# Encoder block on Trainium2: block sums for part of the down projection, and a rearranged output projection

## The chip, the core and the metric

The kernel runs on one core of a Trainium2 chip. A core has TensorE (PE, matrix products into PSUM), VectorE (DVE), ScalarE (ACT), GpSimd (POOL) and SyncE (SP). Each engine works through its own list of instructions in order and waits on semaphores for the others; SP, ACT and POOL also issue DMAs, each on its own queue. The metric is the device time of one execution in microseconds (us), as the median of several runs.

## The reference

One layer of a transformer encoder in fp32: 2048 positions of width 1024. Four heads of differential attention and four groups of Fourier mixing share an input and an output projection, and a gated MLP of width 2816 with a convolution over three positions follows.

```python
h = rmsnorm(x, g_mix[l]);  z = h @ w_in[l]
o_da = diff_attention(q, k, v, lam, slopes)          # from slices of z
o_da = rmsnorm(o_da, g_subln[l], SUBLN_EPS) * (1.0 - lambda_init)
o_ft = fourier_mix(u, w_ft[l])
x = x + concatenate([o_da, o_ft]) @ w_out[l]          # output projection
h = rmsnorm(x, g_ffn[l])
up = centred_dwconv(h @ w_up[l], w_conv[l], b_conv[l])
gate, val = up[..., :D_FF], up[..., D_FF:]
x = x + (jax.nn.silu(gate) * val) @ w_down[l]         # down projection
return rmsnorm(x, g_final)
```

## The kernel before

Every fp32 product is made of three matmuls in the fp32r type. `split` (L79) cuts an operand into a rounded upper part (ACT copy, L83, "hi") and the rest (a subtraction on DVE, or on POOL where `lo_engine` says so, L84, "lo"); `mm3` (L121) then issues hi*hi (L127), hi*lo (L128) and lo*hi (L129). So each operand costs an ACT and a DVE (or POOL) step before PE can use it, and the unit of PE's work is a matmul over 512 columns. A norm is `rstd` and a scaling: ACT squares and sums (L97), POOL adds the epsilon and takes the power (L100, L102), DVE scales (L709 where the result is `hn` or `y`).

The stages follow one another: input projection (to about 330 us), Fourier mixing and attention (to about 985 us), output projection (`out_proj`, L711, to about 1199 us), and the MLP. Positions are cut into 16 blocks (NB) of 128, the 2816 channels into 22 f tiles (NF) of 128.

`out_proj` goes over the 16 blocks. `fetch` brings the mixed rows (mt) and their head scales (fr), `load` multiplies them on POOL (L733) and splits the two halves (ms), lo of the one on POOL, of the other on DVE; `half` makes the products with w_out (tiles wo, wo_x) and adds the residual x (L753); `close` normalises the block before, `transposes` turns the result (hn) by PE (L766) between two groups of matmuls, and ACT stores it to `htd` in DRAM. The weights w_out are split in `out_weights`, lo on DVE, from the end of attention on. `scale_rows` turns the head scales (fs, from POOL at L635) by a PE transpose (L701) and puts them into DRAM for `fetch`; for the last four blocks this is called at block 1. From block 9 on, `b_pieces` (L848) runs beside it in steps: it loads the transposed rows again (hb), forms the block sums that the up projection needs (`sums`, L822 to L825, on POOL), splits them into operands (b) and stores two of the sums (bd).

The up projection is done by block sums (the Strassen-Winograd scheme): a 2 x 2 block product takes 7 products, p1 to p7, instead of 8. Positions go in two groups of 1024. For each group and each f tile there are 7 products of 4 x 3 matmuls = 84. The seven sums of the activations (the b slots, `bops`) are made once per group; the sums of the weights (`sums`, L816 to L819, on DVE) are made for each tile. Products are added up in PSUM banks a, c and d, which other engines read between two products. Convolution, SiLU and the product of gate and value follow, and the result goes to `gd` in DRAM, laid out as [f tile][channel][position].

The down projection is plain. A round handles 512 positions: for each of the 22 f tiles, w_down's rows (512 KB) and the gate columns (256 KB) are loaded, split (tiles d), and multiplied for 4 blocks x 2 column halves, 24 matmuls in 8 PSUM banks that stay open over the round (`down_mm`). At its end `down_out` loads the residual (y<-x2d, L1025), adds it (L1028), normalises and stores to the output (L1033). A round is 528 matmuls, and there are four.

What sets the order: `ffn` lists slots (products and f tiles): up group 0, down round 0, up group 1, down rounds 1, 2, 3. `flow` (L1046) walks through them and issues splits up to three slots ahead and loads a little further, into a ring of 9 operand tiles and two stage tiles. The operands of up group 1 are made by `b_part` during round 0. The last 8 f tiles of round 3 (`LATE`) are prepared in the then unused b slots, and their products run bank by bank, so that the blocks finish one after the other. A scheduler then orders each engine's list by its own model, and the program runs these lists as they are.

Of the kernel before, what the change touches and what calls it, by code (L numbers as in the profile page):

```python
# [40 lines left out]
class Block:  # L41
# [3 lines left out]
    def __init__(self, ctx, tc, a):  # L45
# [22 lines left out]
        self.gd = dt("gd", [NF, P, S], F32)  # L68
# [445 lines left out]
    def out_weights(self, sp, slot, kb, part=0, tag="wost"):  # L514
# [196 lines left out]
    def out_proj(self, pieces):  # L711
# [3 lines left out]
        with ExitStack() as es:  # L715
# [14 lines left out]
            def load(tb):  # L730
# [3 lines left out]
                for half in (1, 0):  # L734
                    m2 = p.tile([P, 4, 2, P], F32R, tag="ms", bufs=4, name=f"ms{tb}_{half}")
                    self.split(mt[:, 4 * half:4 * half + 4], m2[:, :, 0, :], m2[:, :, 1, :],
                               lo_engine=nc.gpsimd if half else None)
# [5 lines left out]
            def half(tb, half, between=None):  # L743
# [8 lines left out]
                self.mm3(ps, [term(kb) for kb in range(H)], first=False)  # L752
                return nc.vector.tensor_tensor(x2[:, c], ps, x2[:, c], ALU.add)  # L753

            def close(tb):
                ms, x2 = ready.pop(tb)
                hn = p.tile([P, D], F32, tag="xh", bufs=4, name=f"hn{tb}")
                self.norm(p, hn, x2, gffn, f"h{tb}", hn)
# [19 lines left out]
            load(0)  # L778
            for _ in self.out_weights(w, lambda: w.tile([P, 1, 2, D], F32R, name="wo3"), H - 1, tag="g"):
# [3 lines left out]
            for tb in range(NB):  # L783
                if tb + 2 < NB:
                    fetch(tb + 2)
                transposes = close(tb - 1) if tb > 0 else None
                half(tb, 0)
                if tb == 1:
                    self.scale_rows(p, pst.tile([P, HALF], F32, tag="tp", name="fsr"), H - 1, NB - 4)
# [17 lines left out]
    def sums(self, pool, blocks, name, eng, last=False):  # L807
# [4 lines left out]
        new = lambda n: pool.tile([P, HALF], F32, tag="sum", bufs=3, name=f"{name}_{n}")  # L812
        t1, t2, t4 = new("t1"), new("t2"), new("t4")
        tt = eng.tensor_tensor
        if not last:
# [16 lines left out]
    def b_part(self, grp, kb, out):  # L832
# [3 lines left out]
        st = self.stage(f"hb{grp}_{kb}")  # L836
        t0 = grp * S // 2
        for half in range(2):

            nc.sync.dma_start(  # L840
                st[:, half::2], self.htd[kb + 4 * half, :, t0:t0 + S // 2].rearrange("p (n t) -> p n t", n=2))
        x11, x21, x12, x22 = (st[:, i] for i in range(4))

        t1, t2, t3, t4 = self.sums(self.sp, (x11, x21, x12, x22), f"hs{grp}_{kb}", nc.vector, True)
# [3 lines left out]
    def b_pieces(self, out):  # L848
# [18 lines left out]
        for kb in range(4):  # L867
            x11, x21, x12, x22 = st[kb]
            t1, t2, t3, t4 = self.sums(self.sp, (x11, x21, x12, x22), f"hs0_{kb}", nc.gpsimd, True)
# [5 lines left out]
            nc.sync.dma_start(self.bd[0, :, kb], t3)  # L875
            nc.sync.dma_start(self.bd[1, :, kb], t4)
# [19 lines left out]
    def up_slots(self, grp):  # L896

        out = [(0, "p1")]
        for n in range(NF):
            out += [(n, q) for q in ("p5", "p6", "p2", "p7")]  # L900
            if n + 1 < NF:
                out.append((n + 1, "p1"))
            out += [(n, "p4"), (n, "p3")]
        return [("up", grp, n, q) for n, q in out]

    def load_up(self, grp, n):
# [297 lines left out]
```

## Time and profile before

| | us |
|---|---|
| median of 3 runs | 2544.21 |
| runs, lowest to highest | 2540.18 to 2544.71 |
| profiled execution | 2540.28 |
| span of its trace | 2538.5 |
| output projection, about 985 to 1199 | 214 |
| up group 0, about 1199 to 1615 | 416 |
| down round 0, about 1615 to 1743 | 128 |
| up group 1, about 1743 to 2163 | 420 |
| down rounds 1 to 3, about 2163 to 2530 | 367 |

The profiled execution is one among several; its own time and its span differ by 1.8 us, which lie outside the trace. Stage bounds are read from the trace and are rounded. The first part of the profile's page gives busy time and share of each engine; the rows of windows give busy time by stage; the rows of waits give an engine, what it waited for, the total, the number of times and the longest. A row of a group gives line, engine, operation, output<-input, shape and count, and behind the bar the busy time in us, the mean ns of one, and the idle time ahead of it with what ended it. The clock column is the share of PE's full clock that was granted.

### The profile page before, as it was taken

Reading aid. Unit: us, or ns where it says so; the run is one execution under the profiler, and the core shown is the slowest. Engines: PE = TensorE matmul, PEld = TensorE weight load, DVE = VectorE, ACT = ScalarE, POOL = GpSimd, SP = SyncE. Lnnn points to the kernel's source line nnn. Section 1 sums busy time; section 2 is a strip of 40 time slices with the busy share of each in tenths; the row PEclk is TensorE's granted clock in tenths of the full one; section 3 lists DMA queues with packets and bytes.
Section 4 is the critical chain, followed back from the end, with each engine's and each line's share of the span. In section 5 each row is a group of like instructions: output and inputs, shape, how many; then the busy total and the mean of one; then the engine's idle time right before and its main releaser. Section 6 shows DMA issues by size and latency. Waiting matters only on the chain.

```text
span 2538.5 us, 34822 instructions
## 1 busy us (share of the span) xinstructions
PE 2484.4 (98%) x13037; PEld 2113.0 (83%) x13037; DVE 1668.7 (66%) x2595; ACT 1301.0 (51%) x2036; POOL 716.9 (28%) x792
## 2 busy tenths in 40 slices
PE   9999998999999998989999999999999999999998
PEld 9998877888888887867888888877888888888886
DVE  4533358988889995343977777667878777434443
ACT  6322236888888884333645545445455455333332
POOL 1400014898888885261110110100001000000000
PEclk9999999999999999999999999999999999999999
DMA  7335558343241215675322222444222222546463
GB/s 266 98 121 145 149 153 227 78 76 76 45 104 28 55 34 173 207 231 182 112 83 92 75 83 88 162 161 171 86 89 75 86 90 87 187 143 218 154 204 111
DMA packets 147080, 317.53 MB, mean 125 GB/s; under 512 B 12432, under 2 KB 65760, under 8 KB 140000
## 3 DMA queue, kind: packets, MB, share of 16 engines
q1 hardware_dynamic: 87088, 231.88, 27.0%
q0 software_dynamic: 18816, 37.72, 7.1%
q10 hardware_dynamic: 41008, 45.72, 5.8%
q8 instruction: 102, 1.67, 0.3%
q14 instruction: 66, 0.54, 0.1%
HBM read 231.34 MB, written 83.93 MB: 124 GB/s over the span
## 4 chain that ended last, share of the span: by engine, by line
PE 46%; DVE 2%; DMA 2%; ACT 1%; issue 1%; POOL 0%; SPq 0%; POOLq 0%; ACTq 0%; DVEq 0%
PE pd L127 5%; PE pd L129 4%; PE pd L128 4%; DMA wd<-in_w_down 1%; DVE d L84 1%; DVE b L84 1%; DMA hb<-htd 1%; DMA wd<-gd 0%; PE pu_0a L127 0%; DVE y L1028 0%; PE pu_21a L127 0%; PE pu_21a L129 0%; PE pu_19a L129 0%; PE pu_15a L129 0%; PE pu_7a L127 0%
## 5 line engine op out<-in xcount | busy, mean ns | idle before, releaser
L592 POOL TENSOR_TENSOR z<-z,z 128x1024 f32<-128x1024 f32 x128 | 307.1, 2416 | 0.0
L84 DVE TENSOR_TENSOR d<-wd,d 128x512 fp32r<-128x512 f32 x240 | 156.7, 689 | 206.2 <-ACT d L83 206.1
L570 PE MATMUL s<-k,q 128*128 128x512 f32 x1024 | 281.4, 396 | 3.0 <-DVE mn L575 2.1
L579 ACT ACTIVATE z<-z,mn 128x2048 f32<-128x2048 f32 x128 | 257.5, 2012 | 33.3 <-DVE mn L575 31.9
L83 ACT ACTIVATE d<-wd 128x512 fp32r<-128x512 f32 x240 | 141.8, 626 | 230.3 <-PE pd L129 170.6
L127 PE MATMUL pd<-d,d 128*128 128x512 f32 x640 | 249.6, 390 | 2.9 <-ACT d L83 2.0
L129 PE MATMUL pd<-d,d 128*128 128x512 f32 x640 | 249.1, 390 | 0.3 <-DVE d L84 0.3
L128 PE MATMUL pd<-d,d 128*128 128x512 f32 x640 | 249.4, 390 | 0.0
L570 PEld LDWEIGHTS s<-k,q 128*128 128x128 f32 x1024 | 174.6, 188 | 29.2 <-DVE mn L575 5.1
L575 DVE CUSTOM_DVE_ANT_0 z<-s,dist,mn 128x1024 f32<-128x1024 f32 x128 | 163.8, 1279 | 38.1 <-PE s L570 37.4
L84 DVE TENSOR_TENSOR at<-pt,at 128x512 fp32r<-128x512 f32 x256 | 170.1, 686 | 8.8 <-ACT at L83 8.7
L83 ACT ACTIVATE at<-pt 128x512 fp32r<-128x512 f32 x256 | 147.9, 592 | 50.8 <-PE pt L601 47.5
L601 PE MATMUL pt<-ident,z 128*128 128x128 f32 x1024 | 156.3, 276 | 6.5 <-DVE at L84 5.1
L127 PE MATMUL o<-at,v 128*128 128x256 f32 x512 | 162.1, 317 | 0.0
L575 DVE CUSTOM_DVE_ANT_0 z<-s,dist 128x1024 f32<-128x1024 f32 x128 | 155.8, 1217 | 5.1 <-PE s L570 5.1
L601 PEld LDWEIGHTS pt<-ident,z 128*128 128x128 f32 x1024 | 124.9, 143 | 38.0 <-issue 11.8
L100 POOL TENSOR_SCALAR y_rs<-y_rs 128x1 f32<-128x1 f32 x16 | 6.9, 431 | 514.5 <-ACT sq L97 514.5
L128 PE MATMUL o<-at,v 128*128 128x256 f32 x512 | 146.1, 285 | 0.0
L127 PEld LDWEIGHTS pd<-d,d 128*128 128x128 f32 x640 | 120.2, 188 | 28.8 <-ACT d L83 2.4
L129 PE MATMUL o<-at,v 128*128 128x256 f32 x512 | 143.7, 281 | 0.0
L129 PEld LDWEIGHTS pd<-d,d 128*128 128x128 f32 x640 | 120.2, 188 | 26.1 <-DVE d L84 1.2
L128 PEld LDWEIGHTS pd<-d,d 128*128 128x128 f32 x640 | 120.2, 188 | 25.2 <-DVE d L84 0.3
(1050 smaller groups left out, 6793.3 us busy)
## 6 DMA issues: line engine op xcount, KB each, us to landing
wu<-in_w_up SPq DMA_DIRECT2D x44, 1024.0 KB
wd<-in_w_down SPq DMA_DIRECT2D x88, 512.0 KB
wd<-gd SPq DMA_DIRECT2D x88, 256.0 KB
q<-qd POOLq DMA_DIRECT2D x32, 512.0 KB, 7.0
gd<-t SPq DMA_DIRECT2D x22, 512.5 KB
gd<-t SPq DMA_DIRECT2D x22, 511.5 KB
wst<-in_w_in SPq DMA_DIRECT2D x72, 128.0 KB
xt<-in_xt SPq DMA_DIRECT2D x16, 512.0 KB
```

The lines of the kernel that those rows point to most:

```text
L83: r = nc.scalar.activation(hi, src, AF.Copy)
L84: return r, (lo_engine or nc.vector).tensor_tensor(lo, src, hi.bitcast(F32), ALU.subtract)
L100: nc.gpsimd.tensor_scalar(t[:, 1:2], t[:, 0:1], 1.0 / D, EPS, ALU.mult, ALU.add)
L127: mm(ah, bh, start=first and i == 0, stop=False)
L128: mm(ah, bl, start=False, stop=False)
L129: r = mm(al, bh, start=False, stop=last and i == n - 1)
L570: nc.tensor.matmul(ps[:, j * HALF:(j + 1) * HALF], qt[:, 2 * c + l, i % 4 * P:i % 4 * P + P], kt[:, c, k0:k0 + HALF], start=l == 0, stop=l ...
L575: nc.vector.tensor_tensor_reduce(zt[:, half * 1024:(half + 1) * 1024], ps, dist[:, d0:d0 + 1024], SLOPES[h], 3.0e38 if half == 0 else mn[: ...
L579: nc.scalar.activation(zt, zt, AF.Exp, bias=mn[:, 2 * c + 1:2 * c + 2], scale=-1.0, accum_out=ss[:, c:c + 1])
L592: nc.gpsimd.tensor_tensor(z[:, x], z[:, x], z1[:, x], ALU.add)
L601: nc.tensor.transpose(pt[:, j * P:(j + 1) * P], zs[n, 0][:, kb * P:(kb + 1) * P], self.ident)
```

## The change

Three things change.

The down projection keeps the plain scheme for f tiles 0 to 9 (`FT` = 10, slots "fil", four rounds of 10 x 24 = 240 matmuls). Tiles 10 to 21 go by block sums in two chunks of six (`CH`, slots "dn"): a chunk and a pair of position blocks is a round of 7 products with 3 x 3 = 9 matmuls each, 8 rounds a chunk. Here the sums of w_down are the operands that stay in the b slots, made by `b_part` during the plain rounds before (on POOL, staged in the tiles xg and xv), and the sums of the gate columns are made for each round, 384 wide, on DVE. The order of slots is: up 0, fil 0, up 1, fil 1, dn chunk 0, fil 2, dn chunk 1 (pairs 6, 7, 0 to 5), and fil 3 at the end, with nine of its ten tiles prepared in the b slots. A block's rows are now complete only after a plain round and two chunks: partial sums go to `x2d` and are loaded again (`residual`, `leave`). Final norms lie in chunk 1 for blocks 0 to 11 and in fil 3 for the rest. `gd` is laid out as [block][channel][f tile][position], so a gate is stored in pieces of 512 bytes.

In `out_proj`, the lo parts of w_out's first three tiles of the heads and of both halves of ms are made by POOL; the transpose of the last head scales moves from block 1 to block 3, behind that block's matmuls; `b_pieces` makes its sums on DVE, stores bd by ACT's queue, and issues its first loads ahead of the fetches of block 9; the last block's norm is done in two halves.

A tile of 480 bytes is reserved ahead of the last w_out tile, which moves its address.

```diff
-            self.split(st[:, c], wt[:, 0, c], wt[:, 1, c])
+            self.split(st[:, c], wt[:, 0, c], wt[:, 1, c], lo_engine=nc.gpsimd if kb < H - 1 else None)
...
-                               lo_engine=nc.gpsimd if half else None)
+                    self.split(mt[:, 4 * half:4 * half + 4], m2[:, :, 0, :], m2[:, :, 1, :], lo_engine=nc.gpsimd)
...
+            w.tile([P, 120], F32, name="pad")
...
+                if tb == 9:
+                    next(pieces)
...
-                if tb == 1:
-                    self.scale_rows(p, pst.tile([P, HALF], F32, tag="tp", name="fsr"), H - 1, NB - 4)
+                if tb == 3:
+                    self.scale_rows(p, pst.tile([P, HALF], F32, tag="tp", name="fsr"), H - 1, NB - 4, mm)
...
-            t1, t2, t3, t4 = self.sums(self.sp, (x11, x21, x12, x22), f"hs0_{kb}", nc.gpsimd, True)
+            t1, t2, t3, t4 = self.sums(self.sp, (x11, x21, x12, x22), f"hs0_{kb}", nc.vector, True)
...
-            nc.sync.dma_start(self.bd[0, :, kb], t3)
+            nc.scalar.dma_start(self.bd[0, :, kb], t3)
...
+    def exec_fil(self, rnd, n, o):
+        if n == 0:
+            self.bops = [self.b_slot(i, rnd + 1) for i in range(7)]
+        if n % 2 == 0 and n // 2 < (4 if rnd == 0 else self.NK):
+            self.b_part(rnd + 1, n // 2, self.bops)
...
+    def load_dn(self, ch, rnd):
+        f0 = self.FT + self.CH * ch
+        st = self.stage(f"g{ch}_{rnd}")
+        for i in range(2):
+            self.nc.sync.dma_start(st[:, 2 * i:2 * i + 2, :self.NK * P],
+                                   self.gd[2 * rnd + i, :, f0:f0 + self.CH].rearrange("p (k f) c -> p k (f c)", k=2))
+        self.wst["dn", ch, rnd] = st
+        self.x2[ch, rnd] = [self.residual(self.mp, tag, 2, 2 * rnd + i, f"r{ch}_{rnd}{i}")
+                            for i, tag in enumerate(("xg", "xv"))]
...
+    def exec_dn(self, ch, rnd, q, o):
+        ps = self.product(q, key, o, self.NK)
+        xs = self.x2[ch, rnd]
+        adds = {"p1": [(0, 0, ps)], "p6": [(0, 1, ps)], "p2": [(0, 0, ps)], "p4": [(1, 0, ps)], "p3": [(0, 1, ps)],
+                "p7": [(1, 1, ps), (1, 1, self.banks.get((key, "d")))]}.get(q, [])
+        for i, half, v in adds:
+            x = xs[i][:, half * HALF:(half + 1) * HALF]
+            nc.vector.tensor_tensor(x, v, x, ALU.add)
+        if q in ("p4", "p3"):
+            i = int(q == "p4")
+            blk = 2 * rnd + i
+            self.leave(xs[i], blk, ch == 1 and blk < 12, f"{ch}_{blk}")
...
-                slots = self.up_slots(0) + self.down_slots(0) + self.up_slots(1) + [
-                    s for r in (1, 2, 3) for s in self.down_slots(r)][:3 * NF - self.LATE]
+                slots = (self.product_slots("up", 0, range(NF)) + fil(0) + self.product_slots("up", 1, range(NF)) + fil(1)
+                         + self.product_slots("dn", 0, range(NB // 2)) + fil(2)
+                         + self.product_slots("dn", 1, (6, 7, 0, 1, 2, 3, 4, 5)))
```

POOL's list between the last product of attention (z) and the first rows of the output projection, before; wo_x and wo are tiles of w_out, fs the head scales, ms and mt the mixed rows:

```order
L592 TENSOR_TENSOR z_0_10614<-z_0_10614,z_1_10659 128x1024 x2
L633 TENSOR_SCALAR ft_10864<-ft_10864 128x2
L634 TENSOR_TENSOR ft_10864<-ft_10864,mhalf 128x2
L635 TENSOR_TENSOR fs<-ft_10864,rr_10299 128x2
L633 TENSOR_SCALAR ft_10918<-ft_10918 128x2
L634 TENSOR_TENSOR ft_10918<-ft_10918,mhalf 128x2
L635 TENSOR_TENSOR fs<-ft_10918,rr_10506 128x2
L84 TENSOR_TENSOR ms_1_10964<-mt_10955,ms_1_10964 128x4x128
```

And the same place after the change:

```order
L592 TENSOR_TENSOR z_0_10614<-z_0_10614,z_1_10659 128x1024 x2
L84 TENSOR_TENSOR wo_x_10759<-wost_10666,wo_x_10759 128x512 x2
L633 TENSOR_SCALAR ft_10864<-ft_10864 128x2
L84 TENSOR_TENSOR wo_x_10759<-wost_10717,wo_x_10759 128x512
L634 TENSOR_TENSOR ft_10864<-ft_10864,mhalf 128x2
L84 TENSOR_TENSOR wo_x_10759<-wost_10717,wo_x_10759 128x512
L635 TENSOR_TENSOR fs<-ft_10864,rr_10299 128x2
L84 TENSOR_TENSOR wo_10824<-wost_10764,wo_10824 128x512 x2
L633 TENSOR_SCALAR ft_10918<-ft_10918 128x2
L634 TENSOR_TENSOR ft_10918<-ft_10918,mhalf 128x2
L635 TENSOR_TENSOR fs<-ft_10918,rr_10506 128x2
L84 TENSOR_TENSOR ms_1_10964<-mt_10955,ms_1_10964 128x4x128
```

Six splits of w_out stand between z and the first split of the mixed rows; before, they were in DVE's list.

POOL's list in the output projection before, around the third of the four steps of block sums (hs are the sums, h_rs the norm of a block):

```order
L733 TENSOR_TENSOR mt_11861<-mt_11861,fr_11863 128x512
L84 TENSOR_TENSOR ms_1_11899<-mt_11755,ms_1_11899 128x4x128
L822 TENSOR_TENSOR hs_2_t_12163<-hb_2_11959 128x512
L100 TENSOR_SCALAR h_rs<-h_rs 128x1
L102 TENSOR_TENSOR h_rs<-h_rs,mhalf 128x1
L823 TENSOR_TENSOR hs_2_t_12164<-hb_2_11959,hs_2_t_12163 128x512
```

The same step in DVE's list after:

```order
L840 TENSOR_TENSOR hs_2_t_12122<-hb_2_11918 128x512
L711 SCALAR_TENSOR_TENSOR hn_11870<-x_9_11712,h_rs,gffn 128x1024
L841 TENSOR_TENSOR hs_2_t_12123<-hb_2_11918,hs_2_t_12122 128x512
L842 TENSOR_TENSOR hb_2_11918<-hb_2_11918 128x512
L754 TENSOR_TENSOR x_10_11811<-o_0_11877,x_10_11811 128x512
```

The sums have left POOL's list, where a norm stood behind one; in DVE's list the norm's scaling (L711) and the add of the output (L754) stand behind a sum.

DVE's list after the change where the last product round ends and the last plain round begins (L1110 adds a product to the residual, L711 is a final norm's scaling, b are the slots filled for fil 3):

```order
L1110 TENSOR_TENSOR r_51_21824<-psd_5a,r_51_21824 128x512
L1110 TENSOR_TENSOR r_50_21822<-psd_5d,r_50_21822 128x512
L711 SCALAR_TENSOR_TENSOR r_51_21824<-r_51_21824,1_11_rs,gfin 128x1024
L84 TENSOR_TENSOR b_3_22067<-wd_4_22107,b_3_22067 128x512
L711 SCALAR_TENSOR_TENSOR r_50_21822<-r_50_21822,1_10_rs,gfin 128x1024
L84 TENSOR_TENSOR b_3_22067<-wd_4_22107,b_3_22067 128x512 x2
L84 TENSOR_TENSOR b_4_22068<-wd_5_22116,b_4_22068 128x512
```

Before, the eight late tiles were split in the b slots in the middle of a plain round, and nothing else read those slots:

```order
L84 TENSOR_TENSOR d_13_1_21806<-wd_13_21707,d_13_1_21806 128x512
L84 TENSOR_TENSOR b_0_21882<-wd_14_21888,b_0_21882 128x512 x2
L84 TENSOR_TENSOR b_0_21882<-wd_15_21897,b_0_21882 128x512
L84 TENSOR_TENSOR b_1_21883<-wd_15_21897,b_1_21883 128x512 x2
L84 TENSOR_TENSOR b_1_21883<-wd_16_21906,b_1_21883 128x512 x2
```

Now tiles 4 to 9 are split behind the last round's adds and between its two norms.

More of the change, by code (lines that the diff above doesn't have):

```diff
@@ L799, in out_proj, with sums @@
             close(NB - 1)(None)
-    def sums(self, pool, blocks, name, eng, last=False):
+    def sums(self, pool, blocks, name, eng, second=False):
         nc = self.nc
         x11, x12, x21, x22 = blocks
-        new = lambda n: pool.tile([P, HALF], F32, tag="sum", bufs=3, name=f"{name}_{n}")
+        new = lambda n: pool.tile([P, HALF], F32, tag="sum", bufs=3, name=f"{name}_{n}")[:, :x11.shape[-1]]
         t1, t2, t4 = new("t1"), new("t2"), new("t4")
         tt = eng.tensor_tensor
-        if not last:
+        if not second:
             tt(t1, x21, x22, ALU.add)
@@ new lines, in prep_a, with product @@
+        return o
+    def product(self, q, key, o, nk=4):
+        bank = {"p1": "a", "p6": "a", "p7": "a", "p4": "a", "p5": "d", "p3": "d", "p2": "c"}[q]
+        if q in ("p1", "p5", "p2"):
+            self.banks[key, bank] = self.psm.tile([P, HALF], F32, tag="ps", bufs=8, name=f"ps{key}{bank}")
+        ps = self.banks[key, bank]
+        b = self.bops[self.PRODUCTS.index(q)]
+        ov = o.rearrange("p l (k f) -> p l k f", k=4)
+        self.mm3(ps, [(ov[:, 0, k], ov[:, 1, k], b[:, 0, k], b[:, 1, k]) for k in range(nk)],
+                 first=q in ("p1", "p5", "p2"), again=q in ("p6", "p7", "p4", "p3"))
+        return ps
@@ L958, in exec_up @@
             copy(xv[:, c[1]], ps)
-            add(xv[:, c[1]], self.banks[n, "d"])
+            add(xv[:, c[1]], self.banks[f"u{grp}_{n}", "d"])
         elif q == "p4":
@@ new lines, in residual, with leave @@
+    def residual(self, pool, tag, bufs, blk, name):
+        x2 = pool.tile([P, S // 2 + 3], F32, tag=tag, bufs=bufs, name=name)[:, :D]
+        self.nc.sync.dma_start(x2, self.x2d[blk])
+        return x2
+    def leave(self, x2, blk, final, name):
+        nc = self.nc
+        if final:
+            jk = self.sp.tile([P, D], BF16, tag="sum", bufs=3, name=f"sq{name}")
+            self.norm(self.tp, x2, x2, self.gfin, name, jk)
+        nc.sync.dma_start(self.a["y"][blk * P:(blk + 1) * P, :] if final else self.x2d[blk], x2)
@@ L1027, in down_out, with fil_out @@
+    def fil_out(self, rnd, tb, half, x2, final):
         c = slice(half * HALF, (half + 1) * HALF)
[L1028 removed]
+        self.nc.vector.tensor_tensor(x2[:, c], self.dps[tb, half], x2[:, c], ALU.add)
         if half == 1:
[L1030 to L1033 removed]
@@ L1046, in flow @@
     def flow(self, slots):
-        need = [1 if s[0] == "up" else 3 for s in slots]
+        need = [3 if s[0] == "fil" else 1 for s in slots]
         loads = {}
```

180 lines of the change are left out of this document (94 added, 86 removed).

## The prediction

> **What bounds the kernel now.** I read the page's first part, then busy time by stage, then TensorE's (PE's) waits, then the clock in the worst places. The stages of the second table are: up for the first half of the positions, down round 0, down round 1 and down round 2.
>
> ```profile
> span 2538.5 us, 34822 instructions
> PE 2484.4 (98%) x13037; PEld 2113.0 (83%) x13037; DVE 1668.7 (66%) x2595; ACT 1301.0 (51%) x2036; POOL 716.9 (28%) x792
> ```
>
> ```profile
> 1199.00:1615.00 416.00, 416.00 (x1823) 344.45 (x1824) 325.11 (x423) 216.78 (x320) 46.77 (x86) 0.99 0.26 94
> 1615.00:1743.00 128.00, 125.64 (x552) 102.73 (x551) 78.33 (x121) 58.44 (x99) 2.75 (x6) 1.00 0.55 183
> 2163.00:2283.70 120.70, 120.70 (x535) 99.94 (x534) 51.03 (x75) 43.20 (x70) 0.00 (x0) 1.00 0.49 161
> 2283.70:2404.00 120.30, 119.88 (x529) 98.98 (x528) 52.52 (x79) 43.02 (x75) 4.11 (x8) 1.00 0.54 184
> ```
>
> Columns: length, then busy time of PE, weight load, VectorE (DVE), ScalarE (ACT), GpSimd (POOL), clock, DMA share, GB/s. PE is never idle in the third row: 120.70/535 = 0.2256 us for a 512-column matmul, back to back. DVE works 42 to 44% of rounds 1 and 2. So here a matmul taken away is time taken away, until something else takes over. The idle time stands elsewhere:
>
> ```profile
> PE ht L766 <- DVE hn L709: 15.6, 3, 10.3
> PE pt L601 <- DVE at L84: 5.1, 4, 3.6
> PE pb L127 <- DVE f L84: 4.6, 6, 1.5
> PE pu_0a L127 <- ACT xg L949: 2.4, 1, 2.4
> PE pd L127 <- ACT b L83: 2.4, 1, 2.4
> ```
>
> ```profile
> 1119.50:1129.80 10.30, 4.18 (x14) 3.70 (x15) 6.51 (x5) 3.90 (x7) 8.54 (x7) 0.50 0.85 317
> 960.00:990.00 30.00, 23.20 (x152) 21.14 (x151) 17.70 (x28) 15.51 (x28) 18.95 (x20) 0.83 0.41 132
> ```
>
> The longest waits, 10.3 us for a norm in the output projection and 3.6 us at attention's end, cost more than themselves, since the clock falls to 0.50 around them.
>
> **Part 1, fewer matmuls.** Before: 4 rounds of 22 x 24 = 2112. After: 4 rounds of 10 x 24 = 960, and 2 chunks x 8 rounds x 7 products x 9 = 1008. That is 144 fewer: 144 x 0.2256 = -32.5 us.
>
> **Part 2, the output projection.** There POOL made the block sums. The waits of POOL between 1095 and 1135 us, and two groups between 1098 and 1140 us:
>
> ```profile
> POOL hs_t L822 <- DMA hb<-htd: 8.0, 2, 4.9
> POOL h_rs L100 <- ACT hn L97: 3.6, 1, 3.6
> ```
>
> ```profile
> L84 DVE TENSOR_TENSOR b<-hs_t,b 128x512 fp32r<-128x512 f32 x8 | 11.1, 1413 | 9.9 <-ACT b L83 9.9
> ...
> L824 POOL TENSOR_TENSOR hb<-hb 128x512 f32<-128x512 f32 x4 | 6.6, 1644 | 0.1
> ```
>
> Eight groups of the whole trace, for the prices here and below (each row: busy us, mean ns of one, idle before it):
>
> ```profile
> L84 DVE TENSOR_TENSOR d<-wd,d 128x512 fp32r<-128x512 f32 x240 | 156.7, 689 | 206.2 <-ACT d L83 206.1
> ...
> L816 DVE TENSOR_TENSOR ws_t<-wu 128x512 f32<-128x512 f32 x44 | 30.4, 691 | 5.9 <-DMA wu<-in_w_up 4.8
> ...
> L84 POOL TENSOR_TENSOR ms<-mt,ms 128x512 fp32r<-128x512 f32 x16 | 21.5, 1343 | 16.6 <-ACT ms L83 16.6
> ...
> L1028 DVE TENSOR_TENSOR y<-pd,y 128x512 f32<-128x512 f32 x32 | 20.7, 686 | 20.1 <-PE pd L129 19.7 <-DMA y<-x2d 0.4
> L709 DVE SCALAR_TENSOR_TENSOR y<-y,y_rs,gfin 128x1024 f32<-128x1024 f32 x16 | 20.6, 1286 | 19.4 <-POOL y_rs L102 19.4
> ...
> L97 ACT ACTIVATE sq<-y 128x1024 bf16<-128x1024 f32 x16 | 16.9, 1058 | 57.5 <-DVE y L1028 57.4
> ...
> L84 DVE TENSOR_TENSOR f<-pb,f 128x256 fp32r<-128x256 f32 x36 | 14.6, 418 | 8.7 <-ACT f L83 8.5
> ...
> L84 DVE TENSOR_TENSOR wo_x<-wost,wo_x 128x512 fp32r<-128x512 f32 x8 | 10.3, 1301 | 0.0
> ```
>
> A sum on POOL that waits for its load holds the norm's step (L100) queued behind it, and PE waits for that norm. The change puts these sums on DVE, where a sum takes 0.69 us for 1.64, and issues the first loads ahead of the fetches. The 10.3 us and the 4.18 x 0.5 = 2.1 us lost at half clock are the most there is: 12.4. The later pair of loads still follows its buffers, and DVE has four sums more for each of four steps, so I take -9, from 0 to -12.4. At attention's end (960 to 990) PE idles 6.8 us and the clock is 0.17 short, up to 5.1 us: 11.9 in all. DVE's splits of w_out (wo_x above, 1301 ns) stood in front of PE's there. A row of POOL's queue there, its wait in brackets:
>
> ```profile
> 983.71 0.19 POOL L633 TENSOR_SCALAR ft<-ft 128x2 f32<-128x2 f32 x1 [6.56 <-DVE ft L632]
> ```
>
> Six such go to POOL, and fsr's transpose goes behind later matmuls. POOL does them between its last head product and the first split of the mix: 6 x 1.34 (the row of ms) to 1.64 = 8.1 to 9.8 us, 6.6 us of it into that waiting. What is over, 1.5 to 3.3 us, delays the first split of the mix if nothing else does: -6, from +3 to -11.9. In the last norm, halving the Square (1.06 us) and the scaling (1.29) takes at most half of each off the chain, 1.2: -1. Together -16, from +3 to -25. The 480-byte pad moves addresses only; no row of before shows an address that matters: 0.
>
> **Part 3, what the two-level rounds add.**
>
> A plain round of before has 66 splits, 8 adds and 4 norms on DVE: 45.5 + 5.5 + 5.1 = 56.1 by these rows, against 52.5 in its window: factor 0.94, since neighbours overlap.
>
> A product round is 63 matmuls, 14.2 us. DVE: 7 splits and 4 sums of 384 columns, halfway between 0.418 and 0.689 = 0.55 each, 6.1; 7 adds, 4.8; and in the six rounds with norms 2 x 1.29: 13.5 x 0.94 = 12.7 us. It fits, but DVE goes in order, and the add that frees a bank for the next product stands behind a norm that waits for ACT and POOL. 0 to 1 us for each of six rounds: +2.5.
>
> The residual's trip: a round's rows go to DRAM or out and the buffer's next rows come in. The add must be done 14.2 us and a product (2.0) after that round's end, 16.2. Add 0.7, norm 4.0 (1.06 and 1.29, POOL's L100 at 0.43, a second POOL step like it or twice as long, and hand-overs), store, load, add 0.7:
>
> ```profile
> L100 POOL TENSOR_SCALAR y_rs<-y_rs 128x1 f32<-128x1 f32 x16 | 6.9, 431 | 514.5 <-ACT sq L97 514.5
> ```
>
> ```profile
> 2286.61 2.33 SPq L1033 DMA_DIRECT2D out_y<-y  x2
> 2289.26 0.33 SPq L1025 DMA_DIRECT2D y<-x2d  x1
> ```
>
> ```profile
> q<-qd POOLq DMA_DIRECT2D x32, 512.0 KB, 7.0
> ...
> hb<-bd POOLq DMA_DIRECT2D x2, 1024.0 KB, 8.1
> ```
>
> The store frees its buffer 2.65 us after issue; a load takes 7.0 at most by the row of that size: 5.4 + 2.65 + 7.0 = 15.1. Hidden, by 1.1 us: cost 0.
>
> Plain rounds are 54.1 us of PE. In the first, DVE has 30 + 28 splits and 8 adds, 45.5 x 0.94 = 42.7 us, in the next two 37.9. But 16 sums on POOL run beside it, and the rows above show what that does: 1413 ns for a split that takes 689. 16 x 0.72 = 11.6 more makes 54.3, the whole cover: +2 (0 to 4). The Trainium skill, "SBUF — State Buffer", section "Who interferes with whom", says more: a DVE instruction with two SBUF inputs and a GpSimd one that reads SBUF shut each other out, the second waiting until the first is done. By that each POOL sum would cost DVE its whole length. The 1413 ns agree in kind; whether in size, no run here shows yet, so the sum by it is a rival, B.
>
> Changes of kind: seven for four. Two old ones left PE 2.4 us idle each (the pu_0a and pd waits); three more at half of that: +3.6 (0 to 7.2).
>
> The last round prepares ten f tiles in slots that the last products still read. After its last add DVE still has 18 splits and 2 norms, 15.0 x 0.94 = 14.1 us; PE has 44 ready matmuls, 9.9 us, and more as tiles arrive, if they do so in the order of PE's list. If PE has to wait for the difference it is +4.2; if tiles come two at a time with 7.0 us of load and 2.1 of splits, six tiles take 27.3 us, 9.9 and 8.1 (three tiles on four banks) of it covered: +9. I take +4.
>
> The gate stores in 512-byte pieces fall in stages with DMA at 0.26: 0, and the end of the kernel (add, norm, store) is as before.
>
> Sum: -32.5 - 16 + 2.5 + 2 + 3.6 + 4 = -36.4, from the profiled execution's 2540.3: 2503.9. The median of the runs shown is 3.9 above that execution; I lay half of it on: 2506.
>
> **Rivals.** A, the output projection only moves its waits. Sums and norms then share DVE's queue, PE still waits about 10 us for a norm. For it: the 8.0 us were waits for loads, whose data come from the same transposes. Against: 0.69 for 1.64 us, and earlier loads. Gives back 16: 2506 + 16 = 2522.
>
> B, DVE becomes the bound in the plain rounds beside POOL. Each of 40 sums takes its 1.64 us from DVE: first round 42.7 + 26.2 = 68.9 against 54.1, +14.8; the others 37.9 + 19.7 = 57.6, +3.5 each. 21.8 in place of the +2: 2526. For it: 1413 ns. Against: a split doubled is not one blocked by 1.64.
>
> C, slower: the residual's trip is late. If store and load each take T, a round with norms loses 5.4 + 2T - 16.2, one without (trip 1.4 + 2T) loses 2T - 14.8: 6 and 10 rounds, 32T - 213. It eats the 36.4 from T = 7.8 us. At 8.1 (the megabyte's row; a round queues 1.8 MB on SP at once) it is 46: 2552. Against: 2.65 us for the store.
>
> D, nothing of Part 3 costs, and Part 2 comes as summed: 2506 - 12 = 2494.
>
> That the matmuls aren't fewer can't be: they are counted from the loops.
>
> The Trainium skill, "TensorE: Matmul & The Clock Gate", Part 1, says that an idle window of about 3.4 us halves the clock until a busy window has passed; the 0.50 row agrees. By it, any of the new stalls that reaches that length adds up to 1.7 us.
>
> **Numbers.** A measurement of this kernel can tell about 0.2%, 5.1 us, from no change. Forecast 0.47, A 0.17, B 0.18, C 0.07, D 0.11. Low end 2489 (D, and the lower bounds of Part 2), high end 2532 (B, and the last round's +9). Faster: all but C and a tail of A with B: 0.90; same 0.04; slower 0.06.
>
> **What would show it.** Matmul rows 13037 less about 144; product rounds of 14.2 us with PE idle under 1 us; PE's wait ht <- hn under 4 us; DVE in the first plain round near 54 us; a wait of about 4 us at the last round's start. Wrong: a wait of psd or L1110 on x2d in every round (C), splits of b over 1.4 us with PE waiting (B), ht <- hn still at 10 (A).

## The result and the profile after

The changed kernel takes 2518.8 us (median; 2513.0 to 2522.2) where the kernel before took 2543.4 in the same series: a ratio of 0.9903, 95% interval 0.9889 to 0.9918, or 24.6 us faster. The forecast was 2506 with a range of 2489 to 2532: the direction and the range were right, a third of the expected gain is missing. The profiled execution of the change, at 2513.0, is the fastest of its four, so differences between traces come out a little kinder to it than differences between medians.

The first two lines of the page after:

```profile
span 2511.2 us, 34985 instructions
PE 2456.5 (98%) x12893; PEld 2086.4 (83%) x12893; DVE 1771.0 (71%) x2760; ACT 1298.3 (52%) x2048; POOL 791.8 (32%) x839
```

PE has 144 matmuls fewer, as counted. The span fell by 27.3 us, less than the 32.5 that these alone are worth. DVE and POOL have more to do: 102 and 75 us.

Where the time lies, by windows of the trace after (columns as in the prediction). The eight rows shown are, in order (a plain round here is one of 10 f tiles, 240 matmuls; a change is the stretch in which its matmuls stand between those of the stage before): up group 0; the change from it to the first plain round; the first plain round; the second; the first chunk of product rounds; the third plain round; the second chunk; the last plain round and the end:

```profile
1191.83:1608.20 416.37, 416.37 (x1824) 344.52 (x1825) 324.89 (x423) 217.25 (x321) 47.98 (x86) 0.99 0.28 94
1608.20:1618.10 9.90, 7.19 (x30) 5.29 (x29) 9.49 (x9) 6.20 (x11) 6.36 (x5) 1.00 0.61 170
1618.10:1676.40 58.30, 55.60 (x236) 44.99 (x235) 55.20 (x66) 30.75 (x53) 25.42 (x21) 0.97 0.61 198
...
2100.20:2153.40 53.20, 53.20 (x236) 44.07 (x235) 41.52 (x60) 25.59 (x46) 16.45 (x8) 1.00 0.65 219
2153.40:2264.10 110.70, 110.41 (x487) 91.12 (x486) 79.73 (x140) 30.20 (x57) 0.05 (x1) 1.00 0.66 232
...
2269.60:2327.80 58.20, 55.61 (x236) 44.83 (x235) 45.31 (x63) 26.12 (x47) 15.27 (x10) 0.97 0.63 213
2327.80:2441.40 113.60, 111.75 (x488) 90.74 (x486) 88.51 (x148) 42.14 (x79) 9.23 (x20) 1.00 0.59 208
2441.40:2503.20 61.80, 60.69 (x259) 47.58 (x257) 27.05 (x38) 17.47 (x31) 3.67 (x10) 1.00 0.46 158
```

Two of the first three plain rounds last 58 us where their 235 matmuls need 53, and the second chunk 113.6 us where 486 need 109.6. In the slow first round DVE is busy for 55.2 of 58.3 us, so PE waits for it; in the third it is busy for 45.3 and PE waits all the same, so a share by itself doesn't tell. PE's wait in the first round, and two windows right behind a wait of 2.4 us there and one of 1.7 us in the third:

```profile
PE pd L128 <- DVE d L84: 2.6, 2, 2.4
```

```profile
1658.72:1662.13 3.41, 3.36 (x8) 2.47 (x8) 3.41 (x7) 0.00 (x0) 1.85 (x2) 0.50 0.40 113
2300.42:2303.83 3.41, 3.41 (x10) 2.66 (x9) 3.41 (x6) 0.44 (x1) 0.00 (x0) 0.50 0.93 278
```

The clock is 0.50 for 3.41 us behind each of the two, which is another 1.7 us. So a third of what such a round loses is the clock, and waits shorter than the 3.4 us that the prediction weighed were followed by it. Not every wait is: behind the 2.7 us at the second change (its row above) the clock stays at 1.00.

PE's waits in the output projection, after:

```profile
PE ht L780 <- DVE hn L711: 7.6, 2, 5.4
PE ht L780 <- DVE hn L772: 3.4, 1, 3.4
PE o L129 <- POOL ms L84: 1.4, 1, 1.4
PE psu_0a L127 <- ACT hs L784: 1.2, 1, 1.2
```

The wait of 10.3 us for a norm (hn) has become two, 2.2 and 5.4; the last block's (L772, in halves) is 3.4 for 4.2. The stage from the first matmul of the output projection to the first of the MLP takes 208.3 us for 213.9, and begins 1.5 us earlier. So 7.1 of the span's 27.3 us come from there and from attention's end, and 20 from the MLP.

The output projection of the change in two windows, the second around these waits:

```profile
983.56:1110.00 126.44, 125.02 (x579) 103.43 (x580) 38.22 (x47) 39.20 (x69) 55.60 (x58) 0.99 0.67 217
1110.00:1140.00 30.00, 22.39 (x94) 18.14 (x93) 21.69 (x28) 11.72 (x22) 9.98 (x10) 0.89 0.88 302
```

In the second the DMA engines are busy for 0.88 of the time, at 302 GB/s.

What slows the plain rounds is seen with two engines beside each other. First POOL, then DVE, in the last part of the first plain round:

```profile
1650.36 1.62 POOL L841 TENSOR_TENSOR hs_t<-hb_3xv,hs_t 128x512 f32<-128x512 f32 x1
1651.95 1.74 POOL L842 TENSOR_TENSOR hb_3xv<-hb_3xv 128x512 f32<-128x512 f32 x1
1653.65 1.74 POOL L843 TENSOR_TENSOR hs_t<-hb_3xg,hs_t 128x512 f32<-128x512 f32 x1
```

```profile
1649.06 1.78 DVE L84 TENSOR_TENSOR d<-wd,d 128x512 fp32r<-128x512 f32 x1
1650.76 1.77 DVE L84 TENSOR_TENSOR b<-hs_t,b 128x512 fp32r<-128x512 f32 x1
1652.46 1.78 DVE L84 TENSOR_TENSOR b<-hb_3xg,b 128x512 fp32r<-128x512 f32 x1
1654.16 1.78 DVE L84 TENSOR_TENSOR b<-hs_t,b 128x512 fp32r<-128x512 f32 x1
1655.87 0.68 DVE L84 TENSOR_TENSOR b<-hb_3xg,b 128x512 fp32r<-128x512 f32 x1
1656.47 0.68 DVE L84 TENSOR_TENSOR b<-hb_3xv,b 128x512 fp32r<-128x512 f32 x1
```

While POOL adds, every split on DVE takes 1.78 us, and one follows the other every 1.70 us; as soon as POOL has ended, at 1655.4, the same split takes 0.68. Here the two engines take turns: read so, 0.68 of the 1.74 us that POOL's sum shows are DVE's.

### The profile page after: what moved, and what is told of

It reads as the page before. It is cut to its first block, busy times and chain, and to the rows that moved or that the text cites. A ratio compares the mean times of both kernels' runs of the same rounds, so it can differ in the third digit from the quotient of the medians.

```text
span 2511.2 us, 34985 instructions
## 1 busy us (share of the span) xinstructions
PE 2456.5 (98%) x12893; PEld 2086.4 (83%) x12893; DVE 1771.0 (71%) x2760; ACT 1298.3 (52%) x2048; POOL 791.8 (32%) x839
## 4 chain that ended last, share of the span: by engine, by line
PE 47%; DVE 3%; DMA 2%; ACT 1%; issue 1%; POOL 1%; SPq 0%; ACTq 0%; POOLq 0%; DVEq 0%
PE pd L129 2%; PE pd L127 2%; PE pd L128 2%; DVE b L84 1%; DVE d L84 1%; PE o L128 1%; PE o L127 1%; PE o L129 1%; DMA g<-gd 1%; DMA wd<-gd 0%; PE psu_0a L127 0%; DVE r L1110 0%; PE psu_0a L129 0%; PE psu_0a L128 0%; PE psu_20a L128 0%
## 5 line engine op out<-in xcount | busy, mean ns | idle before, releaser
L128 PE MATMUL pd<-d,d 128*128 128x512 f32 x248 | 98.2, 396 | 4.4 <-DVE d L84 4.4
L129 PE MATMUL pz<-hth,wt 128*128 128x512 f32 x256 | 100.5, 393 | 0.0
L128 PE MATMUL pz<-htl,wt 128*128 128x512 f32 x256 | 100.5, 392 | 0.0
L127 PE MATMUL pz<-hth,wt 128*128 128x512 f32 x256 | 100.4, 392 | 0.0
L127 PEld LDWEIGHTS o<-at,v 128*128 128x128 f32 x512 | 97.7, 191 | 2.7 <-ACT at L83 1.2
L127 PE MATMUL pd<-d,d 128*128 128x512 f32 x248 | 97.9, 395 | 0.9 <-DVE r L1110 0.8
L128 PEld LDWEIGHTS o<-at,v 128*128 128x128 f32 x512 | 97.9, 191 | 0.8 <-DVE at L84 0.5
L129 PE MATMUL pd<-d,d 128*128 128x512 f32 x248 | 97.9, 395 | 0.2
```

Source lines behind the costliest of these rows:

```text
L127: mm(ah, bh, start=first and i == 0, stop=False)
L128: mm(ah, bl, start=False, stop=False)
L129: r = mm(al, bh, start=False, stop=last and i == n - 1)
```

## The experiments

Two theories stood after this reading. The first: POOL's sums shut DVE out, and the plain rounds and the changes of kind pay for it. The second: DVE just has too much to do there, or the sums come too late. For the output projection: the waits left over come from the order on ACT's queue and the sums' tiles, or from the transfers. All times are medians, with the ratio to the kernel before of the same series.

**The two halves of the change.** One kernel is the kernel before with all edits of the output projection (`out_weights`, `scale_rows`, `out_proj`, `b_pieces`); the other is the changed kernel with all of these taken back, the same lines the other way round.

```diff
-            self.split(st[:, c], wt[:, 0, c], wt[:, 1, c])
+            self.split(st[:, c], wt[:, 0, c], wt[:, 1, c], lo_engine=nc.gpsimd if kb < H - 1 else None)
...
+            w.tile([P, 120], F32, name="pad")
...
+                if tb == 9:
+                    next(pieces)
...
-            t1, t2, t3, t4 = self.sums(self.sp, (x11, x21, x12, x22), f"hs0_{kb}", nc.gpsimd, True)
+            t1, t2, t3, t4 = self.sums(self.sp, (x11, x21, x12, x22), f"hs0_{kb}", nc.vector, True)
```

> The kernel before, with the changed output projection alone (all of Part 2 of the prediction: splits of w_out and of the mixed rows on POOL, later transpose of the head scales, block sums on DVE, their stores on ACT's queue, earlier loads, last norm in halves, pad). The prediction's sum: 16 us faster than before. Theory from the trace after (the output projection starts 1.5 us earlier and takes 208.3 us for 213.9): 7 us faster. Rival: the two parts depend on each other, and alone it gives 0 or more than 12.

Measured: 2538.2 against 2544.4 us, ratio 0.9976 (0.9967 to 0.9985): 6 us faster.

> The changed kernel with the output projection of before: Parts 1 and 3 alone. The prediction's sum: 32.5 - 12.1 = 20.4 us faster than before. Theory from the trace after (1311.4 us for the MLP where its 5664 matmuls need 1277.8, 33.6 us lost, against 21.2 before): 20 us faster. Rival: the stall in the output projection delays the first operands of the MLP, and the parts do not add: under 15 or over 25.

Measured: 2524.7 us, 0.9929 (0.9917 to 0.9941): 20 us by the medians, 18 by the ratio. The halves add up to the 24.6 of the whole, within the noise. The forecast's sum for the MLP (20.4) was met; its sum for the output projection (16) was not.

**Sums on DVE.**

```diff
-        t1, t2, t3, t4 = self.sums(self.sp, (x11, x21, x12, x22), f"hs{grp}_{kb}", nc.gpsimd, True)
+        t1, t2, t3, t4 = self.sums(self.sp, (x11, x21, x12, x22), f"hs{grp}_{kb}", nc.vector, True)
```

> The changed kernel with the 40 block sums that are made beside the plain rounds moved from POOL to DVE. Theory 1, a POOL sum shuts out the DVE split beside it (1.78 us for 0.68 in the trace after): DVE gets 40 x 0.6 = 24 us more work but loses about 40 x 1.1 = 44 us of waiting, and the plain rounds and the changes of kind give back 6 to 10 us against the changed kernel (about 2510). Theory 2, DVE is simply short of time there (55.2 us busy of 58.3 in the first plain round): 16 sums more make 66 us of work for 54 of PE, 8 us or more slower than the changed kernel (2527 or more).

Measured: 2498.7 us, 0.9827 (0.9814 to 0.9841): 20 us faster than the change, twice what the first theory expected; the second falls. (The two traces differ by 14.2, 2511.2 for 2497.0, as the change's is its fastest run.) The windows of the first and third plain round of this kernel:

```profile
1616.90:1670.20 53.30, 53.30 (x237) 44.14 (x236) 51.25 (x80) 31.09 (x54) 16.80 (x9) 1.00 0.73 231
2260.30:2313.30 53.00, 53.00 (x236) 43.88 (x235) 42.54 (x72) 26.11 (x47) 0.00 (x0) 1.00 0.70 233
```

PE is never idle in them, and DVE is busy for less time (51.3 and 42.5 us, where it was 55.2 and 45.3) with 14 and 9 instructions more.

The plain rounds are not all of it. At the first change PE waited 2.4 us in the changed kernel, and for ACT, not for DVE. PE's wait, and ACT's list there:

```profile
PE psu_21a L127 <- ACT xv L979: 2.4, 1, 2.4
```

```profile
1609.04 0.63 ACT L83 ACTIVATE b<-hs_t 128x512 fp32r<-128x512 f32 x1 [0.83 <-POOL hs_t L840]
1610.71 0.63 ACT L83 ACTIVATE b<-hs_t 128x512 fp32r<-128x512 f32 x1 [0.52 <-POOL hs_t L841]
1611.24 0.58 ACT L979 ACTIVATE xv<-psu_21a 128x512 f32<-128x512 f32 x1
```

The copy that PE needs (xv) stands behind upper parts (b) that wait for POOL's sums (hs_t). That is not DVE shut out of anything: the sums come too late for ACT. With the sums on DVE the two changes last 7.4 and 7.8 us, for 9.9 and 10.3. The first change, the second and the second plain round of that kernel:

```profile
1609.50:1616.90 7.40, 6.89 (x31) 5.37 (x30) 6.99 (x13) 5.79 (x11) 0.58 (x1) 1.00 0.60 171
2083.60:2091.40 7.80, 6.90 (x31) 5.37 (x30) 7.37 (x13) 6.17 (x11) 0.00 (x0) 1.00 0.57 172
2091.40:2144.70 53.30, 53.30 (x237) 44.14 (x236) 44.88 (x71) 26.96 (x47) 0.00 (x0) 1.00 0.75 250
```

**POOL beside DVE, with nothing waiting for it.** Sooner results or no lock-out? Here DVE keeps the sums and POOL does as many subtractions into a tile (jk) that nothing reads. The kernel's values stay as they are.

```diff
+        for i in range(4):
+            jk = self.sp.tile([P, HALF], F32, tag="jk", bufs=1, name=f"jk{grp}_{kb}{i}")[:, :x11.shape[-1]]
+            nc.gpsimd.tensor_tensor(jk, x11, x12, ALU.subtract)
```

> The changed kernel with its 40 sums beside the plain rounds on DVE, and POOL doing as many subtractions on the same loaded tiles into a tile that nothing reads: DVE's work and every wait for a result are those of the run with sums on DVE, only POOL is busy beside. Theory 1, POOL and DVE shut each other out: splits of 1.7 us return, the plain rounds lose 5 us each again, and most of the 20 us between 2498.7 and 2518.8 is given back: 2510 to 2520. Theory 2, the gain came from results that are ready sooner (0.68 us on DVE for 1.3 to 1.8 on POOL, and no change of engine): the time stays within 3 us of 2498.7.

Measured: 2543.6 us, 1.0001 (0.9992 to 1.001): all 45 us of the gain gone, far beyond either theory. The waits of SP's queue and of ACT in the first plain round tell why this run can't be read by itself:

```profile
SPq L864 <- POOL jk L869: 10.0, 1, 10.0
```

```profile
ACT b L83 <- DMA hb_3xg<-htd: 9.0, 1, 9.0
```

The next load had to wait until POOL let go of the tile that it read, and ACT for that load: the edit had added a wait of its own. So it was made again with POOL reading an operand (b) that stays until the stage ends:

```diff
             self.split(v, o[:, 0, kb], o[:, 1, kb])
+            if o is out[0]:
+                for i in range(4):
+                    jk = self.sp.tile([P, HALF], F32, tag="jk", bufs=1, name=f"jk{grp}_{kb}{i}")
+                    hi = o[:, 0, kb].bitcast(F32)
+                    nc.gpsimd.tensor_tensor(jk, hi, hi, ALU.subtract)
```

> The run with sums on DVE (2498.7), with 40 subtractions of 512 columns on POOL beside the plain rounds, as many as the change had there, but on operands that lie in a slot until the stage ends, into a tile that nothing reads: unlike the run with unread sums, no load waits for POOL to let go of its tile, and nothing else waits for POOL. Theory 1, POOL and DVE shut each other out: splits of 1.7 to 1.8 us return beside them, some 40 x 1.1 us of DVE, and the time rises by 10 to 20 us. Theory 2, the run with unread sums was slow because its loads waited for POOL: the time stays within 3 us of 2498.7 and splits take 0.69 us.

Measured: 2521.0 us, 0.9914 (0.9901 to 0.9928): 22 us slower than without POOL's instructions, as slow as the change. Its first plain round, and DVE in it:

```profile
1616.20:1679.20 63.00, 56.61 (x236) 45.44 (x235) 59.80 (x81) 32.16 (x56) 33.87 (x21) 0.95 0.61 192
```

```profile
1648.15 1.52 DVE L841 TENSOR_TENSOR hs_t<-hb_2xv,hs_t 128x512 f32<-128x512 f32 x1
1649.60 1.52 DVE L842 TENSOR_TENSOR hb_2xv<-hb_2xv 128x512 f32<-128x512 f32 x1
1651.05 1.52 DVE L843 TENSOR_TENSOR hs_t<-hb_2xg,hs_t 128x512 f32<-128x512 f32 x1
```

The instruction that takes 0.68 us takes 1.52, though nobody waits for POOL's subtractions. The lists of PE, DVE and ACT are the same in this trace and in that of the run with sums on DVE, instruction for instruction. So the lock-out is shown, and the mere company of POOL's instructions can cost 22 us.

It isn't always turn by turn. Shortly before, POOL's first subtraction of a row took 10.41 us, and DVE went on beside it at 0.68 us each, without a gap until 1643.7:

```profile
1634.16 10.41 POOL L873 TENSOR_TENSOR jk<-b 128x512 f32<-128x512 f32 x1 [5.42 <-ACT b L83]
```

```profile
1639.38 0.68 DVE L84 TENSOR_TENSOR b<-hs_t,b 128x512 fp32r<-128x512 f32 x1
1639.98 0.68 DVE L84 TENSOR_TENSOR b<-hb_1xv,b 128x512 fp32r<-128x512 f32 x1
```

Where the three kernels spend their time, in us by the windows of their traces:

| | first change | first plain round | second change | second plain round | third plain round |
|---|---|---|---|---|---|
| the change | 9.9 | 58.3 | 10.3 | 53.2 | 58.2 |
| sums on DVE | 7.4 | 53.3 | 7.8 | 53.3 | 53.0 |
| the same, POOL beside | 7.5 | 63.0 | 7.8 | 57.4 | 55.3 |

The second and third plain round of the last kernel:

```profile
2100.60:2158.00 57.40, 54.08 (x237) 43.81 (x235) 48.93 (x70) 27.47 (x49) 21.05 (x8) 1.00 0.68 220
2275.50:2330.80 55.30, 53.57 (x236) 43.70 (x234) 46.23 (x68) 26.75 (x49) 11.17 (x9) 1.00 0.63 209
```

POOL's company alone costs nothing at the changes and 16 us in the three rounds; the rest of its loss lies in the product rounds behind them. The change lost 5 us at the changes, where its sums came too late, and 10 in two rounds. How these 10 divide between the lock-out and late sums, no run tells: in the rounds, too, ACT waits for POOL's sums.

**The output projection: stores of the sums.** First the queue, in the changed kernel; then the tiles, four for three at every use of their tag, in the kernel with the plain rounds' sums on DVE.

```diff
-            nc.scalar.dma_start(self.bd[0, :, kb], t3)
-            nc.scalar.dma_start(self.bd[1, :, kb], t4)
+            nc.sync.dma_start(self.bd[0, :, kb], t3)
+            nc.sync.dma_start(self.bd[1, :, kb], t4)
```

> The changed kernel with the two stores of block sums issued by SP again, not by ACT. Theory 1, the wait of 5.4 us for a norm at 1128 us comes from ACT's queue, which stood from 1118.8 to 1122.5 us behind such a store that waited for a sum: 3 to 6 us faster than the changed kernel. Theory 2, it comes from the transfers themselves (a mean of 309 GB/s between 1108 and 1130 us, with sums whose tile is freed only by such a store): no change within 2 us, and the wait for hn stays at about 5 us.

Measured: 2518.8 us, 0.9908 (0.9894 to 0.9921): no change. PE's wait for these norms is 8.2 us in three pieces, for 7.6 in two. ACT's queue is not the cause.

```diff
-        new = lambda n: pool.tile([P, HALF], F32, tag="sum", bufs=3, name=f"{name}_{n}")[:, :x11.shape[-1]]
+        new = lambda n: pool.tile([P, HALF], F32, tag="sum", bufs=4, name=f"{name}_{n}")[:, :x11.shape[-1]]
```

> The run with sums on DVE (2498.7), with four tiles for sums in rotation where there were three. Theory 1, the wait of 5.2 us for a norm at 1129 us begins with a sum whose tile is freed only when its store has landed (3.8 us on DVE in the trace of the change): 3 to 5 us faster, and that wait goes. Theory 2, the transfers are what is late there: within 1.5 us, and the wait stands with a load as its cause.

Measured: 2498.3 us, 0.9818 (0.9805 to 0.9832), nothing gained against 2498.7, and PE waits 8.8 us for these norms, for 8.2. The waits of DVE between 1110 and 1135 us of the change, and between 1100 and 1140 of this run:

```profile
DVE hs_t L843 <- DMA bd<-hs_t: 3.8, 1, 3.8
DVE hs_t L840 <- DMA hb<-htd: 2.1, 2, 1.2
```

```profile
DVE hs_t L840 <- DMA htd<-hs: 7.8, 1, 7.8
DVE hs_t L840 <- DMA hb<-htd: 2.4, 2, 1.5
```

The wait for the tile is gone, and a longer one for another transfer stands in its place. So the transfers are late here, whichever tile or queue is freed. That they queue for the DMA engines (a share of 0.88 between 1110 and 1140 us) is the likely reason; it was not tested by taking bytes away.

**The steps of block sums as before** (on POOL, stored by SP, loads behind the fetches; sums of the plain rounds on DVE):

```diff
-                if tb == 9:
-                    next(pieces)
...
-            t1, t2, t3, t4 = self.sums(self.sp, (x11, x21, x12, x22), f"hs0_{kb}", nc.vector, True)
+            t1, t2, t3, t4 = self.sums(self.sp, (x11, x21, x12, x22), f"hs0_{kb}", nc.gpsimd, True)
```

> The run with sums on DVE (2498.7), with the steps of block sums in the output projection as before: on POOL, stored by SP, first loads behind the fetches. The prediction's term for this edit: 9 us slower than 2498.7. Theory from the traces (the wait of 10.3 us became two, 2.2 and 5.4, and a half-clock stretch stays): 3 to 5 us slower. Rival: the waits are due to the transfers alone and only move: within 1.5 us.

Measured: 2502.5 us, 0.9835 (0.9822 to 0.9849): 3.7 us slower by the medians, 2 by the ratios, whose intervals overlap. PE waits 12.5 us for the norms, 11.1 in one piece, for 8.2. The edit is worth what the second expectation said, less than half of the forecast's 9.

**The splits back on DVE**, those of w_out and of one half of the mixed rows (sums of the plain rounds on DVE):

```diff
-            self.split(st[:, c], wt[:, 0, c], wt[:, 1, c], lo_engine=nc.gpsimd if kb < H - 1 else None)
+            self.split(st[:, c], wt[:, 0, c], wt[:, 1, c])
...
-                    self.split(mt[:, 4 * half:4 * half + 4], m2[:, :, 0, :], m2[:, :, 1, :], lo_engine=nc.gpsimd)
+                               lo_engine=nc.gpsimd if half else None)
```

> The run with sums on DVE (2498.7), with the lo parts of w_out and of one half of the mixed rows back on DVE. The prediction's term for attention's end: 6 us slower than 2498.7. Theory from the trace after (the first matmul of the output projection came 1.5 us earlier, with as much PE idle time before it as ever): 1 to 2 us slower. Rival: with POOL free of them, DVE and POOL meet less, and it is no slower or faster.

Measured: 2497.7 us, 0.9813 (0.9800 to 0.9826): not slower. The wait at attention's end moved from DVE to POOL in the change (3.3 us for z, 1.4 for ms) and was worth nothing. With the other half's lo part on DVE as well:

```diff
-                               lo_engine=nc.gpsimd if half else None)
+                    self.split(mt[:, 4 * half:4 * half + 4], m2[:, :, 0, :], m2[:, :, 1, :])
```

> The run with the splits of w_out and of one half of the mixed rows back on DVE (2497.7), with the other half's lo part on DVE too, so that POOL only multiplies by the head scales beside it. Theory 1, POOL and DVE shut each other out here too: 1 to 3 us faster. Theory 2, DVE has room in the output projection (25 us busy of 52 at its end) and PE waits for transfers: within 1.5 us.

Measured: 2498.0 us, 0.9819 (0.9806 to 0.9833): no difference; the second theory holds. The run at 2497.7 beats both kernels, 2545.1 of its series by 47 us and the change by 21.

**The 480 bytes.** Taken from the run at 2497.7:

```diff
-            w.tile([P, 120], F32, name="pad")
```

> The run at 2497.7 without the tile of 480 bytes ahead of the last w_out tile. The prediction: 0, within 1.5 us. Rival: the address matters to PE or to a load, and the output projection's matmuls (768 in the trace, 0.2256 us apart) are slower by some per cent: 2 to 8 us slower.

Measured: 2500.5 us, 0.9833 (0.9819 to 0.9846): 2.8 us slower, with intervals that overlap. In its trace the matmuls of the output projection start 232 to 235 ns apart (medians, by w_out tile), with the pad 227. All the traces agree: 227 in the eleven kernels that have the pad, 232 to 235 in the three that have not. The pad alone, put into the kernel before:

```diff
+            w.tile([P, 120], F32, name="pad")
             for _ in self.out_weights(w, lambda: w.tile([P, 1, 2, D], F32R, name="wo3"), H - 1, tag="g"):
```

> The kernel before with the tile of 480 bytes ahead of the last w_out tile, and nothing else. The prediction: 0. Theory from the trace without the pad (matmuls of the output projection start 232 to 235 ns apart there and before, and 227 ns apart with it): 768 x 5 to 8 ns = 4 to 6 us faster than before, that is most of the 6 us that the whole changed output projection gave. Rival: that spacing follows from other edits beside it: within 1.5 us.

Measured: 2540.2 against 2542.9 us, 0.9988 (0.9979 to 0.9997): 2.7 us faster, less than the 4 to 6 expected. Windows of the kernel before and of this one, 120 us of the output projection without a wait:

```profile
990.00:1080.00 90.00, 90.00 (x418) 73.58 (x417) 28.61 (x36) 27.35 (x49) 27.20 (x32) 1.00 0.68 222
1080.00:1110.00 30.00, 30.00 (x139) 24.49 (x138) 8.94 (x11) 7.94 (x14) 13.38 (x13) 1.00 0.65 210
```

```profile
990.00:1080.00 90.00, 90.00 (x427) 75.11 (x426) 28.81 (x37) 28.37 (x51) 27.25 (x32) 1.00 0.70 221
1080.00:1110.00 30.00, 30.00 (x142) 25.00 (x142) 10.69 (x12) 7.77 (x14) 15.00 (x14) 1.00 0.63 212
```

569 PE instructions for 557 in the same time, with PE at full clock and always busy: 2.2% faster. Over 768 matmuls, 6 ns each, this is 4.6 us. The wait for the norm grew meanwhile (18.8 us in four pieces for 15.6 in three): PE reached the longest of these waits 3.9 us sooner, but left it only 2.7 us sooner.

## Why the prediction was right, and where it was not

Direction and range were right, the account was not: half of rival A and, in kind, rival B came true, and savings that the forecast didn't count made up for a part of them.

Fewer matmuls, -32.5: right. They are gone from the list, and where POOL keeps still the gain comes in full: in the trace of the run with sums on DVE the MLP, from its first to its last matmul, takes 1295.0 us for 1331.4 before, 36.4 less: the 32.5, and 4 more of waiting.

The output projection, -16: wrong, 6 measured alone. Term by term:
- Block sums off POOL, "I take -9": 2 to 4. The step that failed rests on "A sum on POOL that waits for its load holds the norm's step (L100) queued behind it": that moving the sum frees the norm. The queue was the last link, but the load was what came late, and DVE now waits for it with a norm behind it, as rival A said: 7.6 us of waiting where the forecast's sign was under 4. Half of A came true.
- Attention's end, -6: the splits, 0. POOL's waiting of 6.6 us did not hide them; what DVE no longer delayed, POOL's z and ms now delay. The later transpose of the head scales had no run of its own; a wait of 1.7 us for them (fsr on fs) is gone from the trace.
- Last norm in halves, -1: 0.8 by its wait, 3.4 for 4.2.
- The pad, "0": wrong, 2.7 us of the time and 4.6 us of matmul time. The step that failed is "no row of before shows an address that matters": in that trace the down rounds ran at 226 to 227 ns per matmul and the output projection at 232 to 235, and the prediction did not set the two side by side. Block sums (2 to 4) and pad together account for about the 6.

What the MLP adds, +12.1: right in sum (33.6 us lost where before lost 21.2, counting 0.2256 us a matmul: 12.4), wrong in its parts, and the sum came right by luck. Before's round 0, up group 1, and rounds 1 to 3:

```profile
1621.70:1743.90 122.20, 119.84 (x525) 98.08 (x525) 77.10 (x119) 55.07 (x94) 2.17 (x5) 1.00 0.54 181
1743.90:2160.00 416.10, 413.69 (x1825) 342.50 (x1824) 325.38 (x419) 211.39 (x311) 36.80 (x90) 1.00 0.25 91
2166.50:2530.40 363.90, 360.65 (x1581) 297.15 (x1579) 157.99 (x230) 125.93 (x214) 10.35 (x22) 1.00 0.51 171
```

By the same count these rows lose 3.8, 4.4 and 7.2 us. The parts below add up to about 26 us, twice the forecast. To be taken off are the 11 us that before lost in its plain rounds and 3 of the 4.4 in up group 1 (1.5 after), which are gone, and which the forecast had left standing.
- POOL beside the plain rounds, "+2 (0 to 4)": too small. Two plain rounds lost 5 each, and the two changes from up to plain lost 3.4 and 3.8 (9.9 and 10.3 us for 29 matmuls), most of it behind ACT's waits for POOL's sums. All in all POOL costs 20 us, by the two runs that differ in these sums alone. The step that failed is "the whole cover": the round's total of DVE, 54.3, set against PE's 54.1. The total was near, 55.2, but PE waited 2.4 us for one split (d) behind six of b, three of them at 1.78, and the clock fell; the second round, with 8 sums on POOL beside it, lost nothing. This is rival B in kind; B's 21.8 us was near by luck, for it took 1.64 us from DVE for each of 40 sums, all in the plain rounds. Measured, a split that meets a sum is longer by 1.1 us, not every sum meets one, and a part of the cost lies in the changes of kind.
- Changes of kind, +3.6, and norms in the product rounds, +2.5: without POOL beside, the changes cost about 1 us each; the second chunk lost 4.0 us in the change and 4.4 with sums on DVE, the first 1.1 and 0.5. So the norms' term was short by 1 to 2, if all that the second chunk lost is theirs; no run has them alone.
- The last round, +4: 3.4 (56.6 us for 236 matmuls).
- The residual's trip, 0: right. No product round of the change waits for a load of the residual, so rival C has no ground. (The 7.0 us that the forecast took as the most for such a load are the median of another one.) At the ends of the first two plain rounds DVE waits 1.7 and 1.2 us for one, and PE doesn't. DVE's waits in the product rounds are for PE, for ACT's upper parts, for the gate (4.4 us in the first chunk) and for norms, 1 us at most each.

The rule of the Trainium skill that was weighed against the sum, "SBUF — State Buffer", section "Who interferes with whom", was right in kind. The runs with and without POOL's sums agree with it: two inputs in SBUF on both engines, and a split takes 1.78 us for 0.68. In size the sum's own price was nearer, all in all. DVE took 55.2 us for 66 instructions in the first round, where the run with sums on DVE took 51.3 for 80. With 14 fewer at 0.68 that would be 41.8, so the 12 sums that POOL made in that window cost DVE 13 us, 1.1 each. In the second round, by the same reckoning, 8 sums cost it 4 us, 0.5 each. The sum had 0.72; B, which went by the rule, 1.64. What the sum had wrong above all is what it was set against, a spare share of DVE's time in the round; what PE waits for is a single split in a row of them.

## What to carry to other kernels

Before moving work from DVE to POOL to relieve DVE, look for the same instruction in the trace where POOL is busy beside and where it is not: if 0.68 us becomes 1.7, the move can cost DVE more than it saves, and moving it back can be the gain. Look also at who waits for the moved results: an engine that works in order, as ACT here, passes the delay on. Compare the start-to-start time of equal matmuls between stages: a few per cent in one stage alone, with no wait in sight, may be an address. A wait that gives way to another of the same length, when a queue or a tile is freed, can come from the transfers behind both.

## What the runs showed of the hardware that was not expected

A shift of the last w_out tile by 480 bytes took fp32r matmuls over 512 columns from 232 to 235 ns to 227 ns, in two pairs of kernels that differ in it alone (557 and 569 PE instructions in the same 120 us in one of them). Which operand's address does it, and whether a smaller shift would, stays open: the tile's place and everything behind it moved together.

40 instructions on POOL that nobody waits for cost 22 us (2521.0 for 2498.7), on a kernel whose DVE is busy for 51.3 and 42.5 of 53 us in two of the three rounds beside them. DVE can shut POOL out as well: one subtraction of POOL took 10.41 us beside a row of DVE's without a gap, where others took 1.37.

Waits of PE of 2.4 and 1.7 us were each followed by 3.41 us at a clock of 0.50; one of 2.7 us was not.
